# Nine products on zeros ahead of the first operands, gate rows loaded into buffers that are already free, and turned blocks tied behind later products

## The chip, the cores and the metric

The kernel runs on one core of one Trainium2 chip. The metric is the device time of one execution in microseconds (us); lower is better. Inputs and outputs are fp32.

## What is computed

The reference is a transformer of two blocks on 256 latent tokens `x` (256 x 1024) and, in the first block, 256 context tokens `cx`. Cut to what matters here:

```python
def layer(x, cx, c_silu, cctx_silu, norm_w, ada_w, ada_b, w_in, w_out, ...):     # block 1, twice
    shift, scale, gate = jnp.split(mod, 3, axis=-1)        # mod = c_silu @ ada_w + ada_b, likewise mod_c
    hx = rmsnorm(x, norm_w) * (1 + scale[:, None, :]) + shift[:, None, :]
    hc = rmsnorm(cx, norm_w) * (1 + scale_c) + shift_c
    px, pc = split_cols(hx @ w_in), split_cols(hc @ w_in)
    ...                                                     # three kinds of attention: ya, yb, yc_
    ux = jnp.concatenate([ya, yb, yc_], axis=-1) * jax.nn.silu(px[9])
    x = x + gate[:, None, :] * (ux @ w_out)
    if need_ctx:                                            # first layer only
        cx = cx + gate_c * (uc @ w_out)
```

The second block normalises `x` and runs, for each of two layers, a gated feed-forward (ffn1), a mixing stage with attention (mix), and another feed-forward (ffn2).

## The kernel before

**Products.** Every fp32 operand is split into a high part in the fp32r format and a low remainder, and every product is made of three (`three`, L453): high by high, high by low, low by high. Weights stream in tiles of 512 KB on the queue of SyncE (SP), in one fixed order called the wall; ScalarE (ACT) writes the high part `wh` (L291) and VectorE (DVE) the low part `wl` (L292). TensorE (PE) accumulates in PSUM banks `acc`. A scheduler fixes the order of each engine's instructions when the kernel is built, from priorities and its own plan of costs; each engine then works its list strictly in that order. `tc.issue_after(ins)` keeps what is emitted inside it behind the instruction `ins` on the same engine.

**Start of the first layer** (`start`, `quarter`). `x` and `cx` are normalised by rows (`norm_rows`: squares on ACT, then on DVE the root and the scaled copy `xn`, L851). The modulation columns are computed in four quarters. For each, `ada_pair` multiplies the conditioning by a piece of `ada_w` (fp32 products in four column groups at once, `psm`, L446), `ada_cols` copies the result on ACT and turns it into columns (`psr`, L792), DVE adds bias and weight (L805, L808). `turn_pair` transposes two 128-column blocks of `xn` on PE into a PSUM bank `psx` (L859). `mod_pair` then applies scale and shift: ACT reads the bank into `ht` (L868), DVE casts to the high part (L871) and subtracts to the low one (L872), both parts called `hT`. With two k blocks of `hT` ready, the first gate columns of `w_in` are multiplied: 4 accumulators x 3 products = 12 products for each k block, two k blocks (`a == 0` and `a == 1`) for each quarter, so 24 products a quarter and 96 in all. The code emits the next quarter between the two halves, and the scheduler pulls it as far forward as it likes.

**End of a layer** (`layer1`). The attention output `u` is multiplied by `w_out` in two column halves `ct`; `add` multiplies the accumulators by the gate row `gt` (DVE, L1168) and adds to `x` (L1169). In the first layer the context goes through `w_out` as well: `uc` is split first, and its products reuse PSUM banks that `add` frees. `gt` is a tile in a pool that opens only after the attention's pools have closed; its DMA is issued on ACT's queue.

**Second block.** `b2_half(i, h)` turns half `h` of `x` for stage `i` (transposes L496, then `xt_half`: ACT L503 and DVE L504) and takes its squares. For the first stage, `first_scale` (L1555) multiplies `x` in place after both halves have been turned. At later stages a hook at the fourth k step of the first gemm turns half 1; at the first one both halves are turned straight after their columns of `w_out`.

Of the kernel before, what the change touches and what calls it, by code (L numbers as in the profile page):

```python
# [11 lines left out]
F32 = mybir.dt.float32  # L12
# [43 lines left out]
ADA_FILL = [[(1, 0), (1, 512)], [(1, 1024), (1, 1536)], [(1, 2048), (1, 2560)], [(0, 2048), (0, 2560)]]  # L56
QUARTERS = 4
GATE_START = 4

# [171 lines left out]
class Body:  # L231
# [93 lines left out]
    def q(self, cost):  # L325
        self.later = [[a - 1, f] for a, f in self.later]
        due = [f for a, f in self.later if a < 0]
        self.later = [x for x in self.later if x[0] >= 0]
        for f in due:
            f()  # L330
        self.budget = min(self.budget + cost * self.ratio, 4000.0)
        while self.budget > 0 and self.lanes:
            if not self.step():
                break
# [118 lines left out]
    def three(self, out, ah, al, bh, bl, start, stop):  # L453
        mm = self.nc.tensor.matmul
        mm(out, ah, bh, start=start, stop=False)  # L455
        mm(out, ah, bl, start=False, stop=False)  # L456
        mm(out, al, bh, start=False, stop=stop)  # L457

    def gemm(self, name, l, cols0, xh, xl, toks, nk, hook=None, tail=0):


        accs = {t: self.acc() for t, _ in toks}
        k = 0
        while k < nk - tail:
            ks, n, h, lo = self.w_next(name, l, cols0)
            for i, kk in enumerate(ks):
                if hook and k in hook:
                    hook[k]()
                c = 0
                for t, m in toks:  # L470
                    m = m or n
                    self.three(accs[t][:, :m], xh[:, kk, t * P:(t + 1) * P], xl[:, kk, t * P:(t + 1) * P],
                               h[:, i, :m], lo[:, i, :m], k == 0, k == nk - 1)
                    c += 3 * max(m, 256) / 2.4
                k += 1
                self.q(c)
        rest = []
        while k < nk:
            ks, n, h, lo = self.w_next(name, l, cols0)
            rest += [(kk, h[:, i, :], lo[:, i, :]) for i, kk in enumerate(ks)]  # L480
# [302 lines left out]

    def ada_cols(self, g):

        nb = len(g["blocks"])
        self.uid += 1
        m = self.junk.tile([P, 512], F32, tag="junk", name=f"mod{self.uid}")
        self.nc.scalar.copy(m, g["bank"])
        p = self.ps("r")  # L790
        for j in range(4):
            self.nc.tensor.matmul(p[:, 16 * j:16 * j + 2 * nb], m[:, j * P:(j + 1) * P], self.cst("sel2")[:, :2 * nb],  # L792
                                  start=True, stop=True)
        return p[:, :64].rearrange("p (j b s) -> p s b j", b=8, s=2)

    def ada_quarter(self, i):
# [5 lines left out]
        pv = self.ada_cols(g)[:, :, 0, :]  # L802
        for a, j in ((8, 0), (0, 2)):
# [58 lines left out]
    def mod_pair(self, l, s, c, src, hT):  # L862

        nc = self.nc
        self.uid += 1
        tmp = self.junk.tile([P, 2, 256], F32, tag="junk", name=f"ht{self.uid}")
        for i in range(2):
            nc.scalar.activation(tmp[:, i, :], src[:, i, :], AF.Identity, scale=self.mod[l][:, s, 8 + c + i:9 + c + i],  # L868
                                 bias=self.mod[l][:, s, c + i:c + i + 1])
        hi, lo = (h[:, c:c + 2, 256 * s:256 * s + 256] for h in hT)  # L870
        nc.vector.tensor_copy(hi, tmp)  # L871
        nc.vector.tensor_tensor(lo, tmp, hi.bitcast(F32), op=ALU.subtract)  # L872
# [20 lines left out]
    def start(self, x, cx, hT, xp):  # L893
# [16 lines left out]
        def quarter(i):  # L910
            self.ada_quarter(i)
            for s, v in enumerate((xn, cn)):
                self.mod_pair(0, s, 2 * i, self.turn_pair(v, 2 * i), hT)

        quarter(0)
        self.gate_acc = [self.acc() for _ in range(GATE_START)]
        for i in range(QUARTERS):
            ks, _, wh, wl = self.w_next("w_in", 0, 3072)
            for a, kk in enumerate(ks):
# [3 lines left out]
                if a == 0 and i + 1 < QUARTERS:  # L923
                    quarter(i + 1)

# [3 lines left out]
    def layer1(self, l, x, cx, hT, hp):  # L929
# [3 lines left out]
        with ExitStack() as lay:  # L933
# [7 lines left out]
            else:  # L941
# [3 lines left out]
                def sg(c, n, sg2=sg2, cv1=cv1):  # L945
                    return cv1[:, c:c + n, :] if c < 8 else sg2[:, c - 8:c - 8 + n, :]
            att = ExitStack()
            ap = att.enter_context(tc.tile_pool(reuse_waits="tile", name=f"att{l}", bufs=1))
            self.pp = att.enter_context(tc.tile_pool(reuse_waits="tile", name=f"pp{l}", bufs=1))
            self.rawp = att.enter_context(tc.tile_pool(reuse_waits="tile", name=f"raw{l}", bufs=2))  # L950
            self.zp = att.enter_context(tc.tile_pool(reuse_waits="tile", name=f"z{l}", bufs=1))
# [192 lines left out]
            self.until(("attn", 4))  # L1144
            w_out(accs, WOUT_ORDER[:8], first, last, u, 0)
            self.drain()
# [3 lines left out]
            with tc.tile_pool(reuse_waits="tile", name=f"wo{l}", bufs=1) as wp:  # L1150
                gate = wp.tile([P, 2, D], F32, name=f"gt{l}")
                tmp = wp.tile([P, 4, 512], F32, name=f"tmp{l}")
                if need:
# [5 lines left out]
                    nc.sync.dma_start(cx, self.dram["ctx"].rearrange("o (t p) d -> p (o t) d", p=P))  # L1159
                for s in range(2 if need else 1):  # L1160
                    g = self.gates[l][s:s + 1].rearrange("s j p -> s (j p)")
                    nc.scalar.dma_start(gate[:, s, :], g.to_broadcast([P, D]))

                def add(accs, v, s, ct):
                    cs = slice(512 * ct, 512 * ct + 512)
                    for t in range(2):
                        w = tmp[:, 2 * ct + t, :]
                        nc.vector.tensor_tensor(w, accs[t, ct], gate[:, s, cs], op=ALU.mult)  # L1168
                        nc.vector.tensor_tensor(v[:, t, cs], v[:, t, cs], w, op=ALU.add)  # L1169

                for ct in range(2):
                    w_out(accs, WOUT_ORDER[8 + 2 * ct:10 + 2 * ct], first, last, u, 0)
                    add(accs, x, 0, ct)
                    if not need:
                        self.b2_half(0, ct)
                if not need:
# [7 lines left out]
                for ct in range(2):  # L1184
                    w_out(accs, WOUT_ORDER[8 + 2 * ct:10 + 2 * ct], first, last, uc, 2)
                    add(accs, cx, 1, ct)
                self.mod_stream(1, 1, cx, xn, hT)
                return hT
# [356 lines left out]
    def block2(self, x, out):  # L1545
# [18 lines left out]
        for i, (l, s) in enumerate(stages):  # L1564
            ss = first_scale if i == 0 else ops[i][1]
            args = (x, ops[i][0], ss, {4: lambda i=i: self.b2_half(i, 1)} if i else None, lambda h, i=i: self.b2_half(i + 1, h))
            self.psum(s)
# [108 lines left out]
```

## Time and profile before

| | us |
|---|---|
| median of 3 runs | 1901.5 (1901.16 to 1902.7) |
| profiled execution, its own time | 1901.73 |
| its span in the trace | 1899.9 |
| PE busy in the span | 1858.9 (98%) |
| DVE busy | 1228.5 (65%) |
| ACT busy | 1064.7 (56%) |
| granted TensorE clock over the span | 0.997 of full speed |

The span is the part of the execution that the trace covers; the other 1.8 us lie around it. Busy times of engines overlap. Where PE is at 98%, the time can change by idle time of PE, by the clock at which its products run, and by the number of products.

### The profile page before, as it was taken

What the parts mean: (1) busy time and instruction counts of PE and PEld (TensorE: products, weight loads), DVE (VectorE), ACT (ScalarE), POOL (GpSimd) and SP (SyncE); (2) the same over time, 40 slices, a digit from 0 to 9 for tenths busy, and PEclk for the clock granted to TensorE, in tenths of its full rate; (3) what the DMA queues carried; (4) which work ended last, traced back from release to release, by engine and by line L of the source; (5) the groups of instructions that cost most, each with busy time, mean ns of one, the idle gap of its engine ahead of it and who ended that gap; (6) DMA issues with size and microseconds to landing.
All of it is one profiled execution on the core that took longest, in us unless ns stands there. A gap on an engine that the chain in (4) does not pass through costs nothing.

```text
span 1899.9 us, 27515 instructions
## 1 busy us (share of the span) xinstructions
PE 1858.9 (98%) x10348; PEld 1542.5 (81%) x10348; DVE 1228.5 (65%) x2439; ACT 1064.7 (56%) x1941; POOL 4.9 (0%) x14
## 2 busy tenths in 40 slices
PE   6999999999999999999999999999999999999998
PEld 3788788778988877888888878888888888888886
DVE  3466556878586787555798565555555689575555
ACT  3365656875476775444477554444444467645443
POOL 0000000000000000000000000000000000000000
PEclk9999999999999999999999999999999999999999
DMA  8334435245322247554433665555554334555551
GB/s 333 110 106 155 128 92 145 67 166 179 122 87 92 78 149 265 182 188 135 129 107 119 237 217 190 184 172 191 187 187 166 117 103 128 199 178 184 182 188 67
DMA packets 85668, 295.14 MB, mean 155 GB/s; under 512 B 10144, under 2 KB 10656, under 8 KB 85536
## 3 DMA queue, kind: packets, MB, share of 16 engines
q1 hardware_dynamic: 80304, 282.34, 44.7%
q10 hardware_dynamic: 5136, 11.04, 1.9%
q8 instruction: 81, 1.33, 0.3%
q14 instruction: 51, 0.42, 0.1%
q0 software_dynamic: 96, 0.01, 0.1%
HBM read 292.30 MB, written 1.06 MB: 154 GB/s over the span
## 4 chain that ended last, share of the span: by engine, by line
PE 93%; DVE 4%; DMA 2%; ACT 1%; issue 1%; ACTq 0%; DVEq 0%
PE acc L455 25%; PE acc L457 25%; PE acc L456 24%; PE pso L446 4%; PE pst L609 4%; PE pss L543 2%; PE pss L544 2%; PE psr L746 1%; PE psx L1231 1%; DVE wl L292 1%; PE psr L752 1%; PE acc L446 1%; PE psm L1313 1%; DMA ws<-in_wall 1%; ACT wh L291 1%; DMA gt<-gates 1%
## 5 line engine op out<-in xcount | busy, mean ns | idle before, releaser
L292 DVE TENSOR_TENSOR wl<-ws,wh 128x1024 fp32r<-128x1024 f32 (+2 forms) x498 | 589.4, 1185 | 441.2 <-ACT wh L291 440.0
L291 ACT CAST wh<-ws 128x1024 fp32r<-128x1024 f32 (+2 forms) x498 | 508.0, 1023 | 508.0 <-PE acc L457 481.5
L455 PE MATMUL acc<-wh,xt 128*128 128x512 f32 (+3 forms) x1120 | 416.5, 375 | 1.6 <-ACT wh L291 1.6
L456 PE MATMUL acc<-wl,xt 128*128 128x512 f32 (+3 forms) x1120 | 415.6, 372 | 1.4 <-DVE wl L292 1.4
L457 PE MATMUL acc<-wh,xt 128*128 128x512 f32 (+3 forms) x1120 | 415.2, 372 | 0.0
L456 PEld LDWEIGHTS acc<-wl,xt 128*128 128x128 f32 x1120 | 211.1, 188 | 34.1 <-DVE wl L292 2.9
L455 PEld LDWEIGHTS acc<-wh,xt 128*128 128x128 f32 x1120 | 210.6, 189 | 34.2 <-ACT wh L291 2.3
L457 PEld LDWEIGHTS acc<-wh,xt 128*128 128x128 f32 x1120 | 210.7, 189 | 32.5 <-issue 0.7
L455 PE MATMUL acc<-wh,hT 128*128 128x384 f32 (+2 forms) x480 | 159.2, 332 | 0.0
L456 PE MATMUL acc<-wl,hT 128*128 128x384 f32 (+2 forms) x480 | 158.9, 331 | 0.0
L457 PE MATMUL acc<-wh,hT 128*128 128x384 f32 (+2 forms) x480 | 158.3, 330 | 0.0
L579 ACT ACTIVATE p<-pss,nm 128x512 f32<-128x512 f32 (+2 forms) x240 | 127.5, 540 | 32.5 <-DVE nm L562 10.4
L455 PE MATMUL acc<-wh,hffn 128*128 128x512 f32 x352 | 137.9, 392 | 0.0
L457 PE MATMUL acc<-wh,hffn 128*128 128x512 f32 x352 | 137.2, 390 | 0.0
L456 PE MATMUL acc<-wl,hffn 128*128 128x512 f32 x352 | 137.1, 390 | 0.0
L609 PE MATMUL pst<-consts,p 128*128 128x128 f32 x624 | 102.0, 277 | 0.8 <-ACT pt L625 0.8
L455 PEld LDWEIGHTS acc<-wh,hT 128*128 128x128 f32 x480 | 90.8, 189 | 5.6 <-issue 0.4
L457 PEld LDWEIGHTS acc<-wh,hT 128*128 128x128 f32 x480 | 90.7, 189 | 5.1 <-issue 0.8
L456 PEld LDWEIGHTS acc<-wl,hT 128*128 128x128 f32 x480 | 90.8, 189 | 4.9
L609 PEld LDWEIGHTS pst<-consts,p 128*128 128x128 f32 x624 | 72.6, 140 | 25.6 <-ACT pt L625 5.1
L601 ACT ACTIVATE p<-p,rinv 128x256 f32<-128x256 f32 (+2 forms) x152 | 81.4, 576 | 13.3 <-DVE rinv L595 9.4
L457 PEld LDWEIGHTS acc<-wh,hffn 128*128 128x128 f32 x352 | 66.1, 188 | 13.9
(298 smaller groups left out, 2786.7 us busy)
## 6 DMA issues: line engine op xcount, KB each, us to landing
ws<-in_wall SPq DMA_DIRECT2D x476, 512.0 KB, 3.5
ws<-in_wall SPq DMA_DIRECT2D x64, 384.0 KB, 3.1
bias<-in_bias ACTq DMA_DIRECT2D x8, 512.0 KB, 4.1
cx<-in_ctx SPq DMA_DIRECT2D x2, 1024.0 KB, 8.0
ws<-in_wall SPq DMA_DIRECT2D x4, 420.0 KB, 3.1
gt<-gates ACTq DMA_DIRECT2D x3, 512.0 KB, 6.2
x<-in_x SPq DMA_DIRECT2D x1, 1024.0 KB, 6.6
out<-y SPq DMA_DIRECT2D x2, 512.0 KB, 2.7
```

The costliest lines, as they stand in the source:

```text
L291: self.nc.scalar.copy(h[:, :n], s[:, :n])
L292: self.nc.vector.tensor_tensor(lo[:, :n], s[:, :n], h[:, :n].bitcast(F32), op=ALU.subtract)
L446: return self.nc.tensor.matmul(out, a, b, start=start, stop=stop)
L455: mm(out, ah, bh, start=start, stop=False)
L456: mm(out, ah, bl, start=False, stop=False)
L457: mm(out, al, bh, start=False, stop=stop)
L543: nc.tensor.matmul(S[:, o:o + w], q, kh, start=True, stop=False)
L544: nc.tensor.matmul(S[:, o:o + w], q, kl, start=False, stop=True)
L579: nc.scalar.activation(p[:, o:o + w], S[:, o:o + w], AF.Exp, bias=nm[:, i:i + 1], accum_out=sm[:, i:i + 1])
L601: nc.scalar.activation(p[:, o:o + w], p[:, o:o + w], AF.Copy, scale=r[:, i:i + 1])
L609: nc.tensor.transpose(t[:, i * P:(i + 1) * P], sl["P"][:, o:o + P], self.ident)
L746: nc.tensor.transpose(p[:, 2 * a + g, :], ks[:, t, a, g, :], self.ident_r)
```

## The change

It has six parts. (1) `warm(9)`: a tile of zeros from the pool `junk` (two buffers, also used for squares and for `ht`), set by DVE, and nine fp32 products 128x512 on it into a PSUM bank of the kind `pso`, emitted after the normalisation and ahead of quarter 0. (2) Within a quarter the transposes are emitted between the `ada` products and `ada_cols`, whose bank becomes a `pso` one; each later quarter is tied behind the last product of the half before it. (3) `mod_pair` has ACT write the high part straight from PSUM, while DVE computes the full value from the same PSUM bank into `ht` and then subtracts; DVE's cast is gone. (4) The gate rows lie in buffers of the pool `raw`, and their DMA is issued between the fourth and fifth tile of `w_out`. (5) Hooks and due deferred pieces are tied behind the product emitted last (`behind`); for the first stage of block 2, half 0 is turned behind the first piece of `ct = 1`, and half 1 becomes a hook at k step 4 like elsewhere. (6) The context rows for layer 1 are normalised in place and their `mod_pair` calls are deferred.

```diff
@@ start @@
         def quarter(i):
-            self.ada_quarter(i)
-            for s, v in enumerate((xn, cn)):
-                self.mod_pair(0, s, 2 * i, self.turn_pair(v, 2 * i), hT)
-
+            turned = []
+            self.ada_quarter(i, lambda: turned.extend(self.turn_pair(v, 2 * i) for v in (xn, cn)))
+            for s, v in enumerate(turned):
+                self.mod_pair(0, s, 2 * i, v, hT)
+
+        self.warm(WARM)
         quarter(0)
...
                 if a == 0 and i + 1 < QUARTERS:
-                    quarter(i + 1)
+                    self.behind(lambda: quarter(i + 1))
+
+    def warm(self, n):
+
+        z = self.junk.tile([P, 512], F32, tag="junk", name="zeros")
+        self.nc.vector.memset(z, 0.0)
+        p = self.ps("o")
+        for _ in range(n):
+            self.nc.tensor.matmul(p, z[:, :P], z, start=True, stop=True)
@@ three @@
-        mm(out, al, bh, start=False, stop=stop)
+        x = mm(out, al, bh, start=False, stop=stop)
+        self.last_mm = getattr(x, "ins", x)
+
+    def behind(self, f):
+
+        with self.tc.issue_after(self.last_mm):
+            f()
@@ mod_pair @@
         for i in range(2):
-            nc.scalar.activation(tmp[:, i, :], src[:, i, :], AF.Identity, scale=self.mod[l][:, s, 8 + c + i:9 + c + i],
-                                 bias=self.mod[l][:, s, c + i:c + i + 1])
-        hi, lo = (h[:, c:c + 2, 256 * s:256 * s + 256] for h in hT)
-        nc.vector.tensor_copy(hi, tmp)
+            scale, shift = (self.mod[l][:, s, o + c + i:o + c + i + 1] for o in (8, 0))
+            nc.scalar.activation(hi[:, i, :], src[:, i, :], AF.Identity, scale=scale, bias=shift)
+            nc.vector.tensor_scalar(tmp[:, i, :], src[:, i, :], scale, shift, op0=ALU.mult, op1=ALU.add)
         nc.vector.tensor_tensor(lo, tmp, hi.bitcast(F32), op=ALU.subtract)
@@ layer1 @@
-            w_out(accs, WOUT_ORDER[:8], first, last, u, 0)
+            w_out(accs, WOUT_ORDER[:4], first, last, u, 0)
+
+            self.until(("prep", len(bundles) - 1))
+            gates = []
+            for s in range(2 if need else 1):
+                gates.append(self.rawp.tile([P, 2, 512], F32, tag="raw", name=f"gt{l}_{s}").rearrange("p a d -> p (a d)"))
+                g = self.gates[l][s:s + 1].rearrange("s j p -> s (j p)")
+                nc.scalar.dma_start(gates[s], g.to_broadcast([P, D]))
+            w_out(accs, WOUT_ORDER[4:8], first, last, u, 0)
...
                 for ct in range(2):
-                    w_out(accs, WOUT_ORDER[8 + 2 * ct:10 + 2 * ct], first, last, u, 0)
+                    for i in range(2):
+                        w_out(accs, WOUT_ORDER[8 + 2 * ct + i:9 + 2 * ct + i], first, last, u, 0)
+                        if ct and not i and not need:
+                            self.behind(lambda: self.b2_half(0, 0))
                     add(accs, x, 0, ct)
-                    if not need:
-                        self.b2_half(0, ct)
...
-                self.mod_stream(1, 1, cx, xn, hT)
+
+                self.norm_rows(cx, cx)
+                for c in range(0, KD, 2):
+                    self.defer(c + 1, lambda c=c: self.mod_pair(1, 1, c, self.turn_pair(cx, c), hT))
@@ block2 @@
-            args = (x, ops[i][0], ss, {4: lambda i=i: self.b2_half(i, 1)} if i else None, lambda h, i=i: self.b2_half(i + 1, h))
+            args = (x, ops[i][0], ss, {4: lambda i=i: self.b2_half(i, 1)}, lambda h, i=i: self.b2_half(i + 1, h))
```

What this does to the lists of the engines is not told by the diff alone, since the scheduler orders them. **First place: PE at the very start.** Before, its list begins with the `ada` products of quarter 0 (`psm`), the columns, the transposes of both operands, and then the first gate products (`acc`):

```order
L446 MATMUL psm_215<-ws_113,cst_94 32x512 x2
L446 MATMUL psm_215<-ws_111,cst_94 32x512 x2
L446 MATMUL psm_215<-ws_117,cst_94 32x512 x2
L446 MATMUL psm_215<-ws_115,cst_94 32x512 x2
L792 MATMUL psr_238<-consts,mod_236 128x2 x4
L859 MATMUL psx_246<-consts,xn_0_153 128x128 x4
L859 MATMUL psx_256<-consts,xn_1_154 128x128 x4
L455 MATMUL acc_266<-hT_0_100,wh_228 128x512
```

Now the same place on PE reads as follows; `zeros` is the new tile, and `pso_260` is the bank of the columns:

```order
L868 MATMUL psx_248<-consts,xn_0_153 128x128 x4
L943 MATMUL pso_217<-zeros 128x512 x9
L448 MATMUL psm_227<-ws_113,cst_94 32x512 x2
L448 MATMUL psm_227<-ws_111,cst_94 32x512 x2
L448 MATMUL psm_227<-ws_117,cst_94 32x512 x2
L448 MATMUL psm_227<-ws_115,cst_94 32x512 x2
L868 MATMUL psx_253<-consts,xn_1_154 128x128 x4
L800 MATMUL pso_260<-consts,mod_258 128x2 x4
L457 MATMUL acc_280<-hT_0_100,wh_240 128x512
```

The transposes of the normalised `x` moved to the head of the list, and the nine products on zeros stand behind them and ahead of the `ada` products.

**Second place: DVE in quarter 1**, from the columns (`psr`, now `pso`) to the low parts (`hT_1`). Before:

```order
L805 TENSOR_TENSOR mod_87<-psr_297,cols 128x2x2 x2
L808 SCALAR_TENSOR_TENSOR mod_87<-mod_87,cols 128x2x2
L292 TENSOR_TENSOR wl_288<-ws_130,wh_287 128x1024
L871 CAST hT_0_100<-ht_310 128x2x256
L872 TENSOR_TENSOR hT_1_101<-ht_310,hT_0_100 128x2x256
L871 CAST hT_0_100<-ht_320 128x2x256
L872 TENSOR_TENSOR hT_1_101<-ht_320,hT_0_100 128x2x256
```

And now, on the same engine at the same place:

```order
L814 TENSOR_TENSOR mod_87<-pso_321,cols 128x2x2 x2
L817 SCALAR_TENSOR_TENSOR mod_87<-mod_87,cols 128x2x2
L880 TENSOR_SCALAR ht_329<-psx_309,mod_87 128x256
L880 TENSOR_SCALAR ht_335<-psx_314,mod_87 128x256
L294 TENSOR_TENSOR wl_371<-ws_140,wh_370 128x1024
L880 TENSOR_SCALAR ht_329<-psx_309,mod_87 128x256
L880 TENSOR_SCALAR ht_335<-psx_314,mod_87 128x256
L881 TENSOR_TENSOR hT_1_101<-ht_329,hT_0_100 128x2x256
L881 TENSOR_TENSOR hT_1_101<-ht_335,hT_0_100 128x2x256
```

Two casts became four reads of PSUM, the low part of the next quarter's weight tile (`wl_371`) came to stand among them, and both subtractions are now the last rows.

**Third place: PE at the entry to block 2**, where half 1 of `x` is turned (`psx_8312`, `psx_8321`; before `psx_8203`, `psx_8212`). Before, the first two of its transposes stood straight behind the last product of `w_out`, the other six after eight products of ffn1:

```order
L496 MATMUL psx_8203<-consts,x 128x128
L496 MATMUL psx_8212<-consts,x 128x128
L455 MATMUL acc_8251<-wh_8163,xt_0_8139 128x512
L456 MATMUL acc_8251<-wl_8164,xt_0_8139 128x512
L457 MATMUL acc_8251<-wh_8163,xt_0_8140 128x512
L455 MATMUL acc_8252<-wh_8163,xt_0_8139 128x512
L456 MATMUL acc_8252<-wl_8164,xt_0_8139 128x512
L457 MATMUL acc_8252<-wh_8163,xt_0_8140 128x512
L455 MATMUL acc_8251<-wh_8163,xt_0_8139 128x512
L456 MATMUL acc_8251<-wl_8164,xt_0_8139 128x512
L496 MATMUL psx_8203<-consts,x 128x128 x3
L496 MATMUL psx_8212<-consts,x 128x128 x3
```

Now all eight stand behind 24 products of ffn1 (the last of them is the first row), and the last row below needs the low part `wl_8307`:

```order
L459 MATMUL acc_8259<-wh_8209,xt_0_8186 128x512
L504 MATMUL psx_8312<-consts,x 128x128 x4
L504 MATMUL psx_8321<-consts,x 128x128 x4
L457 MATMUL acc_8418<-wh_8306,xt_0_8185 128x512
L457 MATMUL acc_8419<-wh_8306,xt_0_8185 128x512
L457 MATMUL acc_8258<-wh_8260,xt_0_8185 128x512
L458 MATMUL acc_8258<-wl_8261,xt_0_8185 128x512
L457 MATMUL acc_8259<-wh_8260,xt_0_8185 128x512
L458 MATMUL acc_8259<-wl_8261,xt_0_8185 128x512
L458 MATMUL acc_8418<-wl_8307,xt_0_8185 128x512
```

On DVE the rows around that low part are these (`rstd` the scale of `x`, L1581 the scaling of `x` in place, one token tile each):

```order
L415 SCALAR_TENSOR_TENSOR rstd_8364<-rt_8369,ry_8368 128x2
L1581 SCALAR_TENSOR_TENSOR x<-x,rstd_8364,fw 128x1024
L294 TENSOR_TENSOR wl_8307<-ws_8170,wh_8306 128x1024
L512 SCALAR_TENSOR_TENSOR xt_0_8186<-psx_8312,gfirst,xt_0_8185 128x256
L512 SCALAR_TENSOR_TENSOR xt_0_8186<-psx_8321,gfirst,xt_0_8185 128x256
```

The scaling overwrites what the transposes read, so it stands behind them, and `wl_8307` stands behind the scaling.

## Rows read from the trace of the kernel before

**Rows 1.** Page: busy time of PE, share of the span, instructions.

```profile
PE 1858.9 (98%) x10348; PEld 1542.5 (81%) x10348; DVE 1228.5 (65%) x2439; ACT 1064.7 (56%) x1941; POOL 4.9 (0%) x14
```

**Rows 2.** Waits of PE: total us, times, longest.

```profile
PE psx L496 <- DVE x L1169: 3.7, 3, 1.6
PE acc L455 <- DVE hT L871: 2.8, 2, 1.8
...
PE psx L496 <- DVE x L1516: 0.7, 2, 0.3
...
PE psx L496 <- DVE x L1241: 0.3, 1, 0.3
```

**Rows 3.** Timeline of the start: start us, length us, engine, what, idle before.

```profile
12.92 1.42 DVE L851 TENSOR_SCALAR xn<-x,rstd 128x1024 f32<-128x1024 f32 x2
...
13.20 1.94 PE L446 MATMUL psm<-ws,cst 128*32 128x512 f32 x8 [13.20 <-DMA ws<-in_wall]
...
15.67 1.94 PE L446 MATMUL psm<-ws,cst 128*32 128x512 f32 x8 [0.53 <-DMA ws<-in_wall]
...
18.36 1.87 PE L792 MATMUL psr<-consts,mod 128*128 128x2 f32 x8 [0.76 <-ACT mod L789]
...
20.09 1.95 PE L859 MATMUL psx<-consts,xn 128*128 128x128 f32 x8
...
23.87 2.07 PE L455 MATMUL acc<-hT,wh 128*128 128x512 f32 x4 [1.83 <-DVE hT L871]
...
28.73 0.63 PE L457 MATMUL acc<-hT,wl 128*128 128x512 f32 x1
```

**Rows 4.** Timeline of quarter 1 and the next `ada` group.

```profile
29.28 1.07 PE L446 MATMUL psm<-ws,cst 128*32 128x512 f32 x8
...
30.94 1.07 PE L446 MATMUL psm<-ws,cst 128*32 128x512 f32 x8
...
32.97 0.95 PE L792 MATMUL psr<-consts,mod 128*128 128x2 f32 x8
...
34.23 1.23 DVE L292 TENSOR_TENSOR wl<-ws,wh 128x1024 fp32r<-128x1024 f32 x1
...
36.02 0.69 DVE L872 TENSOR_TENSOR hT<-ht,hT 128x512 fp32r<-128x512 f32 x1
...
36.28 1.07 PE L446 MATMUL psm<-ws,cst 128*32 128x512 f32 x8
```

**Rows 5.** Timeline: the last of the 96 products, and the first after it.

```profile
62.10 0.39 PE L457 MATMUL acc<-hT,wl 128*128 128x512 f32 x1
62.32 0.39 PE L455 MATMUL acc<-wh,hT 128*128 128x512 f32 x1
```

**Rows 6.** Groups by line: busy and mean ns; the weights' cast, reads of PSUM banks.

```profile
L291 ACT CAST wh<-ws 128x1024 fp32r<-128x1024 f32 (+2 forms) x498 | 508.0, 1023 | 508.0 <-PE acc L457 481.5
...
L503 ACT ACTIVATE xt<-psx,cols 128x256 fp32r<-128x256 f32 x40 | 17.5, 473 | 9.7 <-DVE xt L504 6.1 <-PE psx L496 3.3
L504 DVE SCALAR_TENSOR_TENSOR xt<-psx,cols,xt 128x256 fp32r<-128x256 f32 x40 | 17.8, 480 | 1.4 <-ACT xt L503 0.3
```

**Rows 7.** Timeline of the first layer's `w_out`, where `gt` is first used.

```profile
423.05 1.29 DVE L1168 TENSOR_TENSOR tmp<-acc,gt 128x512 f32<-128x512 f32 x2 [0.52 <-DMA gt<-gates]
423.80 0.50 PE L455 MATMUL acc<-wh,uc 128*128 128x512 f32 x1 [2.35 <-DVE tmp L1168]
...
425.33 0.63 PE L455 MATMUL acc<-wh,uc 128*128 128x512 f32 x1
...
428.32 0.56 PE L456 MATMUL acc<-wl,uc 128*128 128x512 f32 x1
```

**Rows 8.** Timeline of the entry to block 2.

```profile
717.23 0.44 PE L496 MATMUL psx<-consts,x 128*128 128x128 f32 x2 [1.01 <-DVE x L1169]
...
722.13 0.41 PE L496 MATMUL psx<-consts,x 128*128 128x128 f32 x2 [1.58 <-DVE x L1169]
...
725.50 0.88 PE L496 MATMUL psx<-consts,x 128*128 128x128 f32 x6 [1.12 <-DVE x L1169]
...
731.36 1.28 DVE L1555 SCALAR_TENSOR_TENSOR x<-x,rstd,fw 128x1024 f32<-128x1024 f32 x1
```

More of the change, by code (lines that the diff above doesn't have):

```diff
@@ L57 @@
 QUARTERS = 4
+WARM = 9
 GATE_START = 4
@@ L329, in q @@
         for f in due:
-            f()
+            self.behind(f)
         self.budget = min(self.budget + cost * self.ratio, 4000.0)
@@ L467, in gemm @@
                 if hook and k in hook:
-                    hook[k]()
+                    self.behind(hook[k])
                 c = 0
@@ L782, in ada_pair, with ada_cols @@
         g["n"] += 1
-    def ada_cols(self, g):
+    def ada_cols(self, g, kind="r"):
         nb = len(g["blocks"])
@@ L789, in ada_cols @@
         self.nc.scalar.copy(m, g["bank"])
-        p = self.ps("r")
+        p = self.ps(kind)
         for j in range(4):
@@ L794, in ada_cols, with ada_quarter @@
         return p[:, :64].rearrange("p (j b s) -> p s b j", b=8, s=2)
-    def ada_quarter(self, i):
+    def ada_quarter(self, i, between):
         nc = self.nc
@@ L801, in ada_quarter @@
             self.ada_pair(g)
-        pv = self.ada_cols(g)[:, :, 0, :]
+        between()
+        pv = self.ada_cols(g, "o")[:, :, 0, :]
         for a, j in ((8, 0), (0, 2)):
@@ L866, in mod_pair @@
         tmp = self.junk.tile([P, 2, 256], F32, tag="junk", name=f"ht{self.uid}")
+        hi, lo = (h[:, c:c + 2, 256 * s:256 * s + 256] for h in hT)
         for i in range(2):
-            nc.scalar.activation(tmp[:, i, :], src[:, i, :], AF.Identity, scale=self.mod[l][:, s, 8 + c + i:9 + c + i],
-                                 bias=self.mod[l][:, s, c + i:c + i + 1])
-        hi, lo = (h[:, c:c + 2, 256 * s:256 * s + 256] for h in hT)
-        nc.vector.tensor_copy(hi, tmp)
+            scale, shift = (self.mod[l][:, s, o + c + i:o + c + i + 1] for o in (8, 0))
+            nc.scalar.activation(hi[:, i, :], src[:, i, :], AF.Identity, scale=scale, bias=shift)
+            nc.vector.tensor_scalar(tmp[:, i, :], src[:, i, :], scale, shift, op0=ALU.mult, op1=ALU.add)
         nc.vector.tensor_tensor(lo, tmp, hi.bitcast(F32), op=ALU.subtract)
@@ L946, in sg @@
                     return cv1[:, c:c + n, :] if c < 8 else sg2[:, c - 8:c - 8 + n, :]
+            self.rawp = lay.enter_context(tc.tile_pool(reuse_waits="tile", name=f"raw{l}", bufs=2))
             att = ExitStack()
@@ L1150, in layer1 @@
             with tc.tile_pool(reuse_waits="tile", name=f"wo{l}", bufs=1) as wp:
-                gate = wp.tile([P, 2, D], F32, name=f"gt{l}")
                 tmp = wp.tile([P, 4, 512], F32, name=f"tmp{l}")
@@ L1159, in layer1 @@
                     nc.sync.dma_start(cx, self.dram["ctx"].rearrange("o (t p) d -> p (o t) d", p=P))
-                for s in range(2 if need else 1):
-                    g = self.gates[l][s:s + 1].rearrange("s j p -> s (j p)")
-                    nc.scalar.dma_start(gate[:, s, :], g.to_broadcast([P, D]))
                 def add(accs, v, s, ct):
@@ L1167, in add @@
                         w = tmp[:, 2 * ct + t, :]
-                        nc.vector.tensor_tensor(w, accs[t, ct], gate[:, s, cs], op=ALU.mult)
+                        nc.vector.tensor_tensor(w, accs[t, ct], gates[s][:, cs], op=ALU.mult)
                         nc.vector.tensor_tensor(v[:, t, cs], v[:, t, cs], w, op=ALU.add)
                 for ct in range(2):
-                    w_out(accs, WOUT_ORDER[8 + 2 * ct:10 + 2 * ct], first, last, u, 0)
+                    for i in range(2):
+                        w_out(accs, WOUT_ORDER[8 + 2 * ct + i:9 + 2 * ct + i], first, last, u, 0)
+                        if ct and not i and not need:
+                            self.behind(lambda: self.b2_half(0, 0))
                     add(accs, x, 0, ct)
-                    if not need:
-                        self.b2_half(0, ct)
                 if not need:
```

1 line of the change is left out of this document (removed).

## The prediction

> **What bounds the kernel now.** I read the page first: PE is busy 1858.9 us of a span of 1899.9 [rows 1], so no other engine sets the time, and all that can move it is the idle time of PE (41 us), the clock of its products, and their number. The waits of PE come next [rows 2]: apart from the start, the largest group is 3.7 us for the rows of `x` at the entry to block 2, and 1.0 us more lies at two other turns of `x`. Then the timeline of the start [rows 3, 4], where PE waits 13.2 us for the first weights and then works in pieces, at the lower of its two clock levels: the `ada` group of 13.20 takes 1.94 us, the same group at 29.28 takes 1.07. The 96 gate products of the start end at about 62.3 [rows 5]. A product of 512 columns takes 0.23 us from start to start at the full clock [rows 5] and 0.43 at the lower one, as in the eight products from 425.33 to 428.32 [rows 7]; by 512 columns these are the levels of 2.4 and 1.2 GHz.
>
> **The price of the zeros.** No row of before shows an fp32 product of 128x512 on all columns. An `ada` group is four such products side by side in four column groups, each in two passes; it takes 1.07 us at the full clock and 1.94 at the lower one, fill included [rows 3, 4]. Four products side by side take about as long as one alone, so I take 0.88 and 1.71 for one, a little below the rows. Nine are 7.9 us at the full clock and 15.4 at the lower.
>
> **When they run.** The order puts them on PE behind the first transposes of `xn`, and ahead of the `ada` products. `xn` is ready at 12.92 + 1.42 = 14.34; four transposes are half of the row of 1.95, so the zeros start at about 15.3 (the memset of the tile has no row; the nearest, a DVE subtraction of as many columns, takes 0.69 [rows 4], and from nothing to that it lies beside the transposes). The operands of the `ada` products had come by 13.20 and 15.67 [rows 3]. So the zeros don't fill a wait for operands: they hold back work that was ready. This is the step on which the forecast rests.
>
> How long they last depends on the clock. In before it rose after 4.5 us of products end to end (423.80 to 428.32), and likewise in the 5.4 us from 23.87 to 29.28 [rows 3, 4, 7]. By that three zeros run low and six high: 15.3 + 3 x 1.71 + 6 x 0.88 = 25.7. Bounds: all high, 23.2; all low, 30.7.
>
> The Trainium skill, "TensorE: Matmul & The Clock Gate", Part 3 (The mechanism), says that matmuls start and end strictly in program order. In the rows quoted here every product starts in its order, and nothing in them shows one that overtakes. By that rule the `ada` products cannot slip past the zeros; without it they would, which is the second rival below.
>
> **From the zeros to the first 12 gate products.** Two `ada` groups at 1.0 each end at 27.7; before, they ended at 15.67 + 1.94 = 17.6. From the end of the second group to the columns on DVE took 34.23 - 32.01 = 2.2 us in quarter 1 (its second group starts at 30.94 and takes 1.07; the split of 34.23 is what follows the columns on DVE [rows 4]), so the scale is there at 29.9. Now ACT and DVE read the same bank in turn: 0.47 and 0.48 each [rows 6]. First high part at 30.4 (first product); all four DVE reads of two banks 4 x 0.48 later, 32.3; the first subtraction 0.69 [rows 4] later, 33.0. Four products fit in between, then eight follow: 33.0 + 8 x 0.23 = 34.8. Before they ended at 28.73 + 0.43 = 29.2 [rows 3]. **Loss so far 5.6 us**, though every product now runs at the full clock, where 12 ran at the lower one.
>
> **Quarters 1 to 3.** Before, PE waited for the high parts twice, 2.8 us in all and 1.8 of it for quarter 0 [rows 2], so about 0.9 later; in quarter 1 the `ada` group of 36.28 was still running when they came [rows 4]. Each quarter is now tied behind the first half of the one before, so from the columns (`pso`) to its own low parts PE has 12 products of the other half and 4 high ones: 16 x 0.23 = 3.6 us. The chain needs, after the columns' products: about 0.35 on DVE (32.97 + 0.95 to 34.23 [rows 4]), two ACT reads 0.95, in quarter 1 the cast of `wh` (1.02 [rows 6]) and `wl_371` (1.23 [rows 4]), which the order puts between the two pairs of reads, 0.95 for the second pair and 0.69: 5.2. That leaves 1.6 us of wait, up to 2.4 with the handoffs between engines (0.05 to 0.1 each). In quarter 2 the same comes from the next weight tile, 1.2 to 2.6; in quarter 3 no weight tile, but two small pieces of the rotation tables, 0.3 to 1.1. Sum 3.1 to 6.1, less the 0.9 of before: **2.2 to 5.2, I take 3.6.**
>
> **The clock in this stage.** Between the columns and the first products PE has 4 products in 4 us, later it waits 2 us twice. After an idle time of 2.35 us at 423.80 the clock was low for eight products [rows 7], 8 x 0.2 = 1.6 us. I count two such falls, 3.3 (bounds 0 and 5). Sum of the start: 5.6 + 3.6 + 3.3 = **+12.5 us** (7.8 to 15.9 with the zeros at 25.7; 2.5 less or 5 more at the bounds of their length). The lost time is not hidden later: PE has no slack to catch up [rows 1].
>
> **Gate rows early.** In layer 0 DVE waited 0.52 us for them, PE 2.35 [rows 7]; the splits of `uc` still stand ahead of `tmp` on DVE, so 0.5 goes and 1.8 stays. If the shorter gap no longer lets the clock fall, 1.6 more. **-1.3** (-0.5 to -2.1).
>
> **Entry to block 2.** Three gaps of 1.01, 1.58 and 1.12 us, 3.7 in all [rows 2, 8]. Now half 0 stands behind 12 products and half 1 behind 24 of ffn1 (5.5 us), while its `x` needs about 2.6 us on DVE after the last product of `w_out` (two pairs like that of 1.29 [rows 7]): all three gaps close. But `wl_8307` now stands behind the scaling of `x`, and this behind the transposes. The scaling takes 1.28 [rows 8], the split 1.22, and PE has six products (1.4 us) until it needs it: a new wait of about 1.0. **-2.7** (-1.7 to -3.7).
>
> **Hooks at the other turns of `x`:** the waits of 0.7 and 0.3 [rows 2] lie where half 1 is turned at a stage's start; behind three more k products they vanish. **-1.0** (0 to -1.0). The context rows (part 6) keep their first transposes where they were; with the other moves in attention I take 0, within 0.5 either way.
>
> **Sum:** +12.5 - 1.3 - 2.7 - 1.0 = +7.5. The profiled execution took 1901.73, 0.2 above the median, so **1909.0 us** (1901.5 + 7.5), +0.4%. A change of under 0.2% (3.8 us) can hardly be told from none here.
>
> **Rivals.**
> - *The clock stays high and the other parts give all.* Zeros as forecast, no fall later, waits of the quarters at their low end: 5.6 + 2.2 = 7.8, less 2.1 + 3.7 + 1.0: 1902.5, no change. For it: the zeros do keep PE busy; against it: the idle times worked out are as long as one at which the clock fell.
> - *The zeros are covered (faster).* The mechanism: the `ada` products go ahead when their operands land at 15.67, and zeros only fill what PE would idle. It decides if the `ada` groups still end near 17.6. Then the first 12 products save 12 x 0.2 = 2.4 at the full clock, the second `ada` group, columns and transposes about 2.4, the quarters add 3.6, the rest gives 5.0: 1895.5. Against it: the order of PE. A variant with the same end is that a product on zeros costs far less than its row.
> - *The clock doesn't rise during the zeros.* They end at 30.7: +5.0, 1914.0. Against it: twice it rose after 4.5 to 5.4 us of dense work.
> - *It falls in every wait of the start.* +1.7: 1910.7, and with all waits at the high end 1912.3.
>
> **How the numbers follow.** Forecast (start +9 to +14) 0.58; all gains and no fall 0.18; covered or far cheaper zeros 0.12; no rise 0.07; falls everywhere 0.05. Predicted 1909.0. The range 1902 to 1914 holds the forecast, the last rival and most of the first. Faster by over 0.2% comes from the covered case, 0.12; no change from the first rival, 0.18; slower from the others, 0.70.
>
> **What would show it.** The 96 products end near 75 instead of 62.3; nine long products on zeros lie between 15.3 and about 25.7, the `ada` groups behind them; PE waits for `hT` and `ht` in quarters 0 to 2, each 1 to 2.5 us; no DMA wait ahead of `tmp`, the psx waits for `x` gone, and one of about 1 us for `wl` at the entry to block 2. I am wrong if the `ada` groups run before 20, or if the zeros take under 5 us together, or if gains after 62 exceed 10 us: then the time is at or below before.

## The result and the profile after

| | before | after |
|---|---|---|
| median, us | 1901.68 (1901.16 to 1902.7, 4 runs) | 1914.15 (1912.86 to 1914.53, 4 runs) |
| ratio to before | | 1.0064 [1.0052, 1.0076] |
| profiled span, us | 1899.9 | 1912.0 |
| mean granted clock | 0.997 | 0.995 |

The change makes the kernel 0.64% slower, 12.2 us by the ratio. The forecast was +7.5 us. The direction and the place are as forecast. The size is at the upper end of the range of 1902 to 1914: the ratio gives 1913.7, and the median of these runs lies just above it.

The page of after has PE busy 6.6 us longer than in [rows 1], and so 5.5 us more idle (the zeros alone are busy for 9.42 us):

```profile
PE 1865.5 (98%) x10366; PEld 1547.1 (81%) x10366; DVE 1236.1 (65%) x2456; ACT 1066.5 (56%) x1941; POOL 4.9 (0%) x14
```

The waits of PE (total us, times, longest) answer to [rows 2]. The waits for the rows of `x` at L496 are gone. In their place stand waits for the low parts of `hT` (L881), for a weight's low part (L294) and for `xt` (L512):

```profile
PE psx L868 <- DVE xn L860: 14.7, 3, 13.9
PE acc L458 <- DVE hT L881: 7.3, 4, 2.6
PE acc L458 <- DVE wl L294: 2.7, 3, 2.0
PE acc L459 <- DVE xt L512: 2.3, 2, 1.2
```

The timeline of after's start and of three later places (start us, length us, engine, what, idle before) answers to [rows 3, 4, 5, 7, 8]:

```profile
15.31 9.42 PE L943 MATMUL pso<-zeros 128*128 128x512 f32 x18
24.66 1.92 PE L448 MATMUL psm<-ws,cst 128*32 128x512 f32 x16
29.91 1.21 PE L457 MATMUL acc<-hT,wh 128*128 128x512 f32 x4 [1.50 <-ACT hT L879]
31.53 1.28 DVE L881 TENSOR_TENSOR hT<-ht,hT 128x512 fp32r<-128x512 f32 x2
32.87 0.79 PE L458 MATMUL acc<-hT,wh 128*128 128x512 f32 x1 [1.75 <-DVE hT L881]
...
36.02 0.63 PE L459 MATMUL acc<-hT,wl 128*128 128x512 f32 x1
36.58 3.03 PE L448 MATMUL psm<-ws,cst 128*32 128x512 f32 x16
...
41.46 0.23 DVE L814 TENSOR_TENSOR mod<-pso,cols 128x4 f32<-128x4 f32 x2 [7.51 <-PE pso L800]
42.52 1.00 DVE L880 TENSOR_SCALAR ht<-psx,mod 128x256 f32<-128x256 f32 x2 [0.69 <-ACT hT L879]
43.91 1.23 DVE L294 TENSOR_TENSOR wl<-ws,wh 128x1024 fp32r<-128x1024 f32 x1 [0.40 <-ACT wh L293]
45.06 0.99 DVE L880 TENSOR_SCALAR ht<-psx,mod 128x256 f32<-128x256 f32 x2
45.96 1.28 DVE L881 TENSOR_TENSOR hT<-ht,hT 128x512 fp32r<-128x512 f32 x2
47.30 0.50 PE L458 MATMUL acc<-hT,wh 128*128 128x512 f32 x1 [2.10 <-DVE hT L881]
...
59.46 0.79 PE L458 MATMUL acc<-hT,wh 128*128 128x512 f32 x1 [2.63 <-DVE hT L881]
71.34 0.50 PE L458 MATMUL acc<-hT,wh 128*128 128x512 f32 x1 [0.83 <-DVE hT L881]
...
437.39 0.50 PE L457 MATMUL acc<-wh,uc 128*128 128x512 f32 x1 [1.74 <-DVE tmp L1190]
439.12 0.39 PE L458 MATMUL acc<-wl,uc 128*128 128x512 f32 x1
439.35 0.40 PE L459 MATMUL acc<-wh,uc 128*128 128x512 f32 x1
...
735.90 0.15 DVE L525 TENSOR_TENSOR ssum<-xss 128x2 f32<-128x2 f32 x1
736.99 1.03 PE L504 MATMUL psx<-consts,x 128*128 128x128 f32 x8
737.95 1.22 DVE L294 TENSOR_TENSOR wl<-ws,wh 128x1024 fp32r<-128x1024 f32 x1
739.28 0.16 DVE L415 SCALAR_TENSOR_TENSOR rstd<-rt,ry 128x2 f32<-128x2 f32 x1
739.54 1.28 DVE L1581 SCALAR_TENSOR_TENSOR x<-x,rstd,fw 128x1024 f32<-128x1024 f32 x1
740.75 1.22 DVE L294 TENSOR_TENSOR wl<-ws,wh 128x1024 fp32r<-128x1024 f32 x1
742.02 0.80 PE L458 MATMUL acc<-wl,xt 128*128 128x512 f32 x1 [2.03 <-DVE wl L294]
...
929.22 0.53 PE L459 MATMUL acc<-wh,xt 128*128 128x280 f32 x2 [1.16 <-DVE xt L512]
```

Windows of after (us; PE, PEld, DVE, ACT, POOL busy and instructions; granted clock; DMA share; GB/s):

```profile
33.00:39.50 6.50, 6.50 (x24) 2.94 (x24) 0.94 (x1) 0.00 (x0) 0.00 (x0) 0.55 1.02 406
...
60.00:63.50 3.50, 3.50 (x16) 2.18 (x18) 0.00 (x0) 0.00 (x0) 0.00 (x0) 0.61 0.24 98
742.00:746.30 4.30, 4.28 (x12) 3.44 (x13) 2.73 (x5) 2.20 (x6) 0.00 (x0) 0.60 1.02 361
```

How to read it: the zeros fill PE from 15.31 to 24.73, and the `ada` groups stand right behind them. Then PE waits 1.50 us, does four products, waits 1.75 us, and the next products start 0.43 us apart: the granted clock of 33 to 39.5 is 0.55 of full, the level of 1.2 GHz. It is back at the full level of 2.4 GHz by 41, and after the wait of 2.63 at 59.46 it falls once more (0.61).

Where the time went is seen best product by product. The kernel has 7248 products made by `three`, the same in both traces, so the k-th of them (counted from 0) can be set side by side. The table is worked out from the start times in the two traces; the last column is what the forecast had for that stretch.

| product | before | after | lag | change of the lag | forecast |
|---|---|---|---|---|---|
| first | 23.87 | 29.91 | +6.0 | | |
| first after the 96 | 62.32 | 76.01 | +13.7 | +13.7 | +12.5 |
| no. 1190 (attention of layer 0) | 419.01 | 433.23 | +14.2 | +0.5 | 0 |
| no. 1300 (gate rows) | 450.31 | 463.24 | +12.9 | -1.3 | -1.3 |
| no. 2400 (layer 1) | 704.98 | 717.53 | +12.55 | -0.4 | 0 |
| no. 2500 (entry to block 2) | 736.22 | 748.71 | +12.5 | 0 | -2.7 |
| last | 1890.38 | 1902.49 | +12.1 | -0.4 | -1.0 |

### The profile page after: what moved, and what is told of

Read it like the earlier page. It is cut to its first block, busy times and chain, and to the rows that moved or that the text cites. A ratio compares the mean times of both kernels' runs of the same rounds, so it can differ in the third digit from the quotient of the medians.

```text
span 1912.0 us, 27558 instructions
## 1 busy us (share of the span) xinstructions
PE 1865.5 (98%) x10366; PEld 1547.1 (81%) x10366; DVE 1236.1 (65%) x2456; ACT 1066.5 (56%) x1941; POOL 4.9 (0%) x14
## 4 chain that ended last, share of the span: by engine, by line
PE 90%; DVE 3%; ACT 1%; DMA 1%; issue 1%; ACTq 0%; DVEq 0%
PE acc L459 24%; PE acc L457 24%; PE acc L458 24%; PE pso L448 4%; PE pst L617 4%; PE pss L551 2%; PE pss L552 2%; PE psr L754 1%; PE psx L1257 1%; DVE wl L294 1%; PE psr L760 1%; PE acc L448 1%; PE psm L1339 1%; DMA ws<-in_wall 1%; ACT wh L293 1%
## 5 line engine op out<-in xcount | busy, mean ns | idle before, releaser
L294 DVE TENSOR_TENSOR wl<-ws,wh 128x1024 fp32r<-128x1024 f32 (+2 forms) x498 | 589.2, 1185 | 441.8 <-ACT wh L293 440.8
```

Source lines behind the costliest of these rows:

```text
L294: self.nc.vector.tensor_tensor(lo[:, :n], s[:, :n], h[:, :n].bitcast(F32), op=ALU.subtract)
```

## The experiments

Each is timed against the kernel before, runs of both taken in turn on one chip; us are the ratio less 1, times 1901.5. Two kernels serve as a base: the changed one, and that of e2 (its start undone). "96 end" is how much later than in before the first product after the 96 starts, in the profiled execution. One such execution can lie off the median of its kernel: that of e8 is 2.7 us below it, that of e4 2.1 us above, so small differences in this column are not told apart.

| kernel | ratio to before | us | 96 end |
|---|---|---|---|
| after | 1.0064 [1.0052, 1.0076] | +12.2 | +13.7 |
| e3 new start alone | 1.0077 [1.0064, 1.0091] | +14.6 | +13.8 |
| e2 old start, all else new | 0.9987 [0.9978, 0.9996] | -2.5 | -1.5 |
| e1 after without zeros | 1.0009 [1.0, 1.0018] | +1.7 | +4.9 |
| e6 zeros alone | 1.0014 [1.0005, 1.0023] | +2.7 | +2.7 |
| e12 after with old `mod_pair` | 1.0018 [1.0009, 1.0027] | +3.4 | +5.6 |
| e8 e1 with old `mod_pair` | 1.0 [0.9991, 1.0009] | 0 | +0.6 |
| e7 e1 with quarters untied | 1.0015 [1.0006, 1.0024] | +2.9 | +5.3 |
| e4 after, zeros at the head | 1.0014 [1.0006, 1.0023] | +2.7 | +6.9 |
| e5 e2 with scaling tied later | 0.9971 [0.9959, 0.9982] | -5.5 | +0.1 |
| e9 e5 and 11 zeros at the head | 0.9964 [0.995, 0.9978] | -6.8 | -2.25 |
| e10 e5 and one hook untied | 0.9968 [0.9956, 0.9981] | -6.1 | 0 |
| e11 e5 and new `mod_pair` | 0.9961 [0.9948, 0.9973] | -7.4 | -2.0 |

**Which part holds the loss: e3 and e2.** e3 is before with parts 1 to 3 of the change, e2 is after with these three undone.

> The kernel before with parts 1 to 3 alone (zeros, order and ties of the quarters, pair of reads). Theory 1: the 96 products end near 76.0 and the kernel takes 1901.7 + 13.7 = 1915.4 us. Rival (part of the loss at the start comes from how parts 4 to 6 shift its order): under 1911.

> The changed kernel with its start as before: no zeros, the order within a quarter, the bank, the pair of reads and the untied quarters of before. Parts 4 to 6 stay. Theory 1 (the loss lies in the start alone, the rest gives 1.6 us): 1900.1 us. Rival (the rest costs time too and only looked like a gain after a delayed start): 1902 or more.

+14.6 and -2.5 give +12.1, and after has +12.2: the start holds all of the loss, and within the intervals the start and the rest simply add. Parts 4 to 6 alone make the kernel faster, by 2.5 us where the forecast's terms had 5.0.

**The zeros: e1, e6, e4.** e1 takes only the zeros out of after:

```diff
-        self.warm(WARM)
         quarter(0)
```

> The changed kernel without the nine products on zeros and their memset. Theory 1 (the zeros hold back ready work): the ada products of quarter 0 end near 21 instead of 26.5, the first 12 gate products near 31 instead of 36.5, and the kernel takes about 1908.5 us, 5 to 6 less than the changed one. Rival (the zeros repay themselves, because what follows them runs at the full clock): within 2 us of the changed kernel, 1912 to 1916.

Without them the kernel is at +1.7: they cost 10.5 us there. That is more than the 5 to 6 expected: the parts of the start don't simply add. By the 96th product after is 8.8 us behind e1, 4.1 of it up to the 12th product and 4.7 behind it. e6 adds `warm(9)` to before and nothing else.

> The kernel before with the nine products on zeros alone, emitted ahead of quarter 0; nothing else changed. Theory 1 (they hold back the ada products by some 9 us; a part comes back by the full clock): the first gate products start near 30.5, the 96 products end 5 to 10 us later than before, 1908 us (1906 to 1911). Rival (alone they cost nothing, only together with the tied quarters): within 2 us of before.

They cost 2.7 us there, not 6 or more. Timeline and windows of e6:

```profile
15.18 10.23 PE L935 MATMUL pso<-zeros 128*128 128x512 f32 x18 [15.18 <-DVE ssum L519]
25.34 1.92 PE L448 MATMUL psm<-ws,cst 128*32 128x512 f32 x16
32.21 1.19 PE L457 MATMUL acc<-hT,wh 128*128 128x512 f32 x4 [0.23 <-DVE hT L873]
```

```profile
25.00:33.00 8.00, 7.01 (x52) 3.23 (x52) 2.63 (x8) 3.94 (x7) 0.00 (x0) 1.00 1.03 410
33.00:66.00 33.00, 32.71 (x179) 23.73 (x178) 14.01 (x33) 13.50 (x23) 0.00 (x0) 1.00 0.36 139
```

Here the zeros hold the `ada` groups back as well (25.34 against 13.20 in [rows 3]), and the first product starts 8.3 us later than before. But the scheduler, free to do so, pulled quarter 1's `ada` products into the wait. PE's longest gap behind the zeros is 0.76 us, the clock stays full, and most of the delay is won back. The Trainium skill, "TensorE: Matmul & The Clock Gate", section "Loop structure matters more than you think", says that the loop nest decides whether products stay warm, by their following one another without a wait. The two traces agree: in e6 PE is busy 32.71 of 33 us and the granted clock is 1.00, and in after it drops to 0.55 and 0.61 behind the waits.

e4 keeps after's zeros, but sets them at the very head of the program, on a tile of their own, where PE has nothing else to do.

> The changed kernel with the zeros in a tile of their own, set at the head of the program, so that the nine products run between 1 and 12 us, while PE waits for its operands anyway. Theory 1 (place decides, not the products themselves): the ada products of quarter 0 end near 19 to 20, the first 12 gate products near 27, and the kernel takes about 1904.5 us, 8 to 10 less than the changed one. Rival (the products themselves or the rest of the new start cost the time wherever they stand): 1912 to 1915.

The time is as expected (+2.7), the reason is not. Timeline and windows of e4:

```profile
1.46 9.79 PE L943 MATMUL pso<-zeros 128*128 128x512 f32 x18 [1.46 <-DVE zeros L940]
```

```profile
16.00:33.00 17.00, 12.04 (x44) 6.62 (x44) 7.81 (x18) 4.50 (x7) 0.00 (x0) 0.52 1.03 411
```

The zeros end at 11.25, PE idles 2.51 us at 13.75 and 1.21 at 17.64, and the clock is at the lower level for the whole stretch in which the first 12 products run. What early zeros give is lost before the gate products could use it; e4 is no better than e1, which has none.

**Which partner makes the zeros dear: e12, e8, e7.** e12 is after with the old `mod_pair` (ACT writes `ht`, DVE casts and subtracts); e8 is the same edit on e1. e7 is e1 with `quarter(i + 1)` called without `behind`.

> The changed kernel with the mod_pair of before; zeros and ties stay. Theory 1 (zeros, tied quarters and pair cost more together than apart, because the waits of the pair let the clock fall again that the zeros had raised): 4 to 7 us less than the changed kernel, 1908.5 us. Rival (the costs simply add, 1.9 us for the pair): 1912.2 us.

> The kernel of e1_no_zeros with the mod_pair of before: ACT alone reads PSUM, DVE casts and subtracts. Theory 1 (the pair that reads one bank in turn gives the low parts later): each quarter's wait for them gets 0.5 us shorter, 1901.5 us. Rival (the new pair is the quicker one): 1903.4 or more.

> The kernel of e1_no_zeros with the quarters no longer tied behind the half before, so that the scheduler may put their ada products and transposes into the wait for the low parts. Theory 1 (tie and pair together cost the 4.9 us that e1 still loses by the end of the 96 products; the tie about half): 1901 us. Rival (the tie costs nothing): 1903.4.

The old `mod_pair` takes 8.8 us off after (12.2 to 3.4), more than the 4 to 7 expected, but only 1.7 off e1, where the two intervals meet. So zeros and new pair together cost 7.1 us more than the two costs added up (12.2 - 3.4 - 1.7 + 0). All four of these kernels have the tie, so they don't tell its share. Untying alone gives nothing: in e7 `ada` groups do move between the first high products and the first low ones, but one wait of 3.42 us stays, at 60.29, with the clock low behind it. Zeros and new pair without the tie were not run.

Where these 8.8 us lie can be read product by product. In the two profiled executions the last products are 10.1 us apart. The 12th product starts at 36.0 in after and at 35.5 in e12, the 96th at 75.8 and 67.7: 7.6 us fall between these two, in quarters 1 to 3. Another 1.6 lie at the entry to block 2, where the clock fell in after and not in e12. DVE's list in quarter 1 of e12, and PE's first product that needs its result:

```profile
39.62 0.23 DVE L814 TENSOR_TENSOR mod<-pso,cols 128x4 f32<-128x4 f32 x2 [6.50 <-PE pso L800]
41.16 0.43 DVE L880 CAST hT<-ht 128x512 fp32r<-128x512 f32 x1 [1.17 <-ACT ht L877]
41.62 0.69 DVE L881 TENSOR_TENSOR hT<-ht,hT 128x512 fp32r<-128x512 f32 x1
42.23 0.42 DVE L880 CAST hT<-ht 128x512 fp32r<-128x512 f32 x1
42.68 0.69 DVE L881 TENSOR_TENSOR hT<-ht,hT 128x512 fp32r<-128x512 f32 x1
42.70 1.20 PE L457 MATMUL acc<-hT,wh 128*128 128x512 f32 x4 [0.26 <-DVE hT L880]
43.29 1.22 DVE L294 TENSOR_TENSOR wl<-ws,wh 128x1024 fp32r<-128x1024 f32 x1
```

From the columns on DVE to the last low part it takes 42.68 + 0.69 - 39.62 = 3.75 us, and `wl` stands behind. In after the same chain is 45.96 + 1.28 - 41.46 = 5.78 us: four reads of PSUM in place of two casts, and `wl` in between. In e1, new pair but no zeros, it is 4.43 (37.37 to 41.80), and `wl` stands behind as in e12:

```profile
37.37 0.23 DVE L814 TENSOR_TENSOR mod<-pso,cols 128x4 f32<-128x4 f32 x2 [7.54 <-PE pso L800]
40.52 1.28 DVE L881 TENSOR_TENSOR hT<-ht,hT 128x512 fp32r<-128x512 f32 x2
41.72 1.22 DVE L294 TENSOR_TENSOR wl<-ws,wh 128x1024 fp32r<-128x1024 f32 x1
```

PE has 16 products, 3.7 us, to cover it. Hence the waits in quarters 1 to 3: 0.26 three times in e12 (there for the high parts, the casts); 1.24, 0.77 and 0.83 in e1; 2.10, 2.63 and 0.83 in after, where quarter 2 has a `wl` in the same place. After against e12, then: 5.6 - 0.8 = 4.8 us of waits, 3.03 - 1.92 = 1.1 for the `ada` pair that runs at the low clock at 36.58, and some 1.6 for the eight products that do so from 59.46 (8 x 0.2): 7.5 of the 7.6. No run moved `wl` alone, so its share of the waits is read from these rows.

**The entry to block 2: e5.** e5 is e2 with `first_scale` tied on DVE behind the low part of the first tile of `wu`:

```diff
+            with tc.issue_after(self.low[self.wi]):
                 r1 = self.finish_rstd(ops[0][1], 2)
...
```

> The kernel of e2_old_start, with the scaling of x in place at the entry to block 2 (and the root and squares around it) tied on DVE behind the low part of the first wu tile. Theory 1 (the gain of closed gaps at the entry to block 2 was eaten by the wait for that low part, 2.0 us, a wait of 0.3 ahead of it, and the lower clock after it, 1.5): these 3.8 us go, 1895.5 us. Rival (the scale for silu comes later instead and PE waits there): 1898.5 or more.

-5.5 against -2.5 for e2. The two intervals meet, but the profile of e5 has the `wl` wait gone and the scaling behind the split:

```profile
729.07 1.22 DVE L294 TENSOR_TENSOR wl<-ws,wh 128x1024 fp32r<-128x1024 f32 x1
730.21 2.48 DVE L1572 SCALAR_TENSOR_TENSOR x<-x,rstd,fw 128x1024 f32<-128x1024 f32 x2
741.02 0.50 PE L458 MATMUL acc<-wh,xt 128*128 128x512 f32 x1 [0.42 <-ACT sffn L1235]
```

Across the entry its products win 3.9 us on before's, where e2's win nothing. About 1.5 of this is the clock, which fell behind the `wl` wait in e2; in e7, e8 and e12, with the same wait and no fall, the products win 1.6 across the entry.

**Can more be had: e9, e10, e11,** all on e5. e9 sets 11 zeros at the head; e10 leaves the hook of the mixing stage's first gemm untied; e11 takes the new `mod_pair`, with the start's old order and no tie.

> The kernel of e5_scale_behind with eleven products on zeros at the head of the program, in a tile of their own, from about 1.4 to 13 us, so that no idle time lies between them and the first ada products; order, ties and pair of the start as before. Theory 1 (zeros pay when they fill idle time without a gap, since ada products, columns, transposes and 12 gate products then run at the full clock): the 96 products end 3 to 5 us earlier, 1893 us. Rival (as with the nine early zeros, the clock falls in the small waits that follow and nothing is left): 1896 to 1898.

> The kernel of e5_scale_behind with the hook of the first gemm of mix not tied, as before. Theory 1 (the new waits of 1.16 us for the low part of xt at both entries to mix come from this tie; before they were 0.34): the two waits shrink, 0.6 to 1.6 us less, 1895.5 us. Rival (they come from the order on DVE whatever the tie): 1896.7, with the waits unchanged.

> The kernel of e5_scale_behind with the new mod_pair alone, quarters untied and in the order of before. Theory 1 (reading one bank in turn with ACT and DVE gives the low parts later and makes PE wait in each quarter): 2 to 4 us more, 1899.5 us. Rival (the pair costs only together with the tied quarters): 1896 to 1897.5.

None can be told from e5, whose interval meets each of theirs. e10 shows that the wait of 1.16 us for `xt` at the mixing stage comes from the tie: in its trace the waits there are 0.32 and 0.34, for `wl` as in before. e11, expected slower than e5, has the lowest median. Lines of its timeline:

```profile
24.76 1.94 PE L449 MATMUL psm<-ws,cst 128*32 128x512 f32 x8
26.63 0.52 PE L459 MATMUL acc<-hT,wh 128*128 128x512 f32 x1
```

Here the scheduler puts quarter 1's `ada` group between the first high products and the first low ones, so PE works while DVE makes the low parts, and all its waits for `hT` together are 1.9 us (2.8 in e5, 8.8 in after). The pair that costs so much in after costs nothing that can be measured here. But e11 has neither the zeros, nor the tie, nor the new order within a quarter; e7, without zeros and tie, has waits of 4.9 us. Which of the three makes the difference is not shown.

## Why the prediction was right, and where it was wrong

**The step on which it rested was right.** The zeros start at 15.31 (forecast 15.3), end at 24.73 (25.7) and hold back `ada` groups that were ready; nothing slips past them. The rivals of covered zeros and of a clock that doesn't rise are out, though the 1914.0 of the latter is the number nearest to the measured one. The clock did fall, but not in every wait: it stayed up behind those of 2.10 and 0.83 at 47.30 and 71.34.

**The first 12 products.** They end at 36.4. The forecast had 34.8 and the clock apart from that; eight of the products ran at the low level, 8 x 0.2 = 1.6, which makes up the difference. That the rest agrees is luck. The zeros ended 1.0 earlier than forecast, since about two of them ran at the lower level and not three. From there to the first low product it took 0.8 longer (8.1 us, forecast 7.3): that product waited for both subtractions (1.28 from 31.53), where the sum had one (0.69).

**Quarters 1 to 3.** The waits sum to 5.6 us, within 3.1 to 6.1, where 3.6 + 0.9 = 4.5 was taken; 1.1 too little. The cause named (the next tile's `wl` between the pairs of reads, in quarters 1 and 2) fits the rows of after, e12 and e1.

**The clock.** Two falls, as counted. They cost 1.6 + 1.6 for products and 1.1 for the `ada` pair between, 4.3 where 3.3 was taken. The waits and the clock are thus 2.1 above the sum, and the start came out only 1.2 above it (+13.7 against +12.5). The other 0.9 was won back in quarters 1 to 3, and the sum had no term for it: between the 12th product and the end of the 96, PE turns from these products to `ada` products, columns or transposes and back ten times in before and four times in after, and in the rows of before each such turn costs some 0.2 us. No run tested this alone.

**The gate rows** gave 1.3 as forecast, in part by luck: no wait for the DMA is left, PE still waits 1.74 for `tmp` (0.6 less), and behind it the products follow 0.23 apart, so the clock doesn't fall (1.6 less). Of these 2.2 a new wait of 0.56 for `xn` at 451.29 takes back a part. The gain from the clock is not certain either: in e6, with the gate rows of before, PE waits 2.94 there and the clock stays up.

**The step that failed is the entry to block 2,** as it was put: "The scaling takes 1.28, the split 1.22, and PE has six products (1.4 us) until it needs it: a new wait of about 1.0", and so -2.7. The three gaps did close. But the scaling didn't start when the transposes were done (738.02). It waited for the scale, `rstd`, the end of a chain of thirteen small DVE operations from 735.90 to 739.44 with a `wl` of 1.22 among them; that chain I had not counted, because in before it lay under other waits. [rows 8] hint at it: there the scaling starts 5.0 us after the last transposes end. The new wait was 2.03, with 0.31 for `wh` ahead of it, and then the clock was at 0.60 for 4.3 us, in which 12 products took 4.28 in place of 12 x 0.23 = 2.8. Together 3.8, and 3.7 had been won: nothing. e5 takes that wait away and the gain appears. The term that was put at nothing is this chain: the new wait alone was twice what was forecast, and the lower clock behind it came on top.

**Hooks.** Of 1.0 us only 0.4 came: the wait of 0.3 at the turn of L1241 is gone, but the other two (0.7 together, L1516) are still there, 0.42 each, ahead of a product in place of a transpose (1131.74 and 1715.94, `x` by L1542). And at the entry to the mixing stage the tied hook holds up the low part of `xt`: 1.16 us at 929.22 and 1.15 at 1513.24, where before had waits of 0.34.

By stretches: start +1.2, attention of layer 0 +0.5, layer 1 -0.4, entry +2.7, hooks +0.6. That is 4.6 us above +7.5, and the trace has +12.1. What made the 0.5 and the -0.4 was not tried.

**What stays open.** Why DVE's list has `wl` between the reads with the zeros and behind them without is a matter of the scheduler's plan, and no run tells. The start's end differs between executions of nearly one program (the starts of e2 and e5 are the same code and end 1.6 us apart in their profiles), with the moment at which the clock rises; so the gains of e9, e10 and e11 over e5 stay unsettled. e9 and e11 together were not run.

## What to carry to other kernels

Work that only warms an engine belongs where that engine has nothing ready, and what follows it must come without a gap: placed ahead of ready products it cost 2.7 us here, 3.4 under the tie with the old pair (e12 against e8), and 10.5 with the new pair, where longer waits followed and the clock fell again. At the head of the program, where PE has nothing to do, it gave no gain clear of the noise either (e4, e9). A change that makes a chain on another engine longer (four PSUM reads for two casts) should be tried with and without each of its companions: the new pair costs 8.8 us beside the zeros, 1.7 without them, and nothing that can be measured in e11. A tie fixes an order and so can keep the scheduler from filling such waits, but that it cost time at the start is not shown here. When a wait closes, look for every input of the next operation, not only the one that the code shows beside it; here it was a chain of thirteen tiny operations, about 0.2 us each.

## What the hardware showed that was not expected

The granted clock of a window has to be checked against the products in it. In e1 the window from 25 to 35 shows 1.00, though the products there start 0.43 us apart, which is the lower level. Window and products of e1:

```profile
25.00:35.00 10.00, 8.32 (x29) 4.17 (x29) 4.65 (x8) 2.28 (x4) 0.00 (x0) 1.00 1.03 410
```

```profile
29.35 0.63 PE L459 MATMUL acc<-hT,wl 128*128 128x512 f32 x1
29.77 0.63 PE L458 MATMUL acc<-hT,wh 128*128 128x512 f32 x1
```

The clock's record in the trace of e1 has its first entry at 33.88, a rise; ahead of it nothing is recorded, and a window there shows 1.00. The first entry is a rise in the other traces as well, so at a start the spacing of like products is the surer sign.

Whether the clock falls behind a wait could not be told from the length of the wait. At the entry to block 2 seven kernels have the same wait of 2.0 us for `wl`. In after, e1, e2 and e4 products behind it start 0.43 us apart, in e7, e8 and e12 they stay at 0.23. Ahead of the gate rows a wait of 2.35 us (before) and one of 2.67 (e3) were followed by the lower level, one of 2.94 (e6) was not. Shorter ones can be enough: 1.50 and 1.75 us with four products between them were followed by it in after. So a term for a fall of the clock in a sum, as in the prediction, is a chance and not a price.
